# Output products of a recurrence grouped by their rows, and an order of TensorE that keeps products on parts of the array together

## The chip, the core and the metric

One Trainium2 chip, of which one core works. TensorE multiplies, VectorE (DVE), ScalarE (ACT) and GpSimd (POOL) do the elementwise work, and SyncE (SP) issues every DMA. The metric is the device time of one launch, in microseconds (us).

## The reference, cut to what matters

The function is one layer of a backbone, in float32, for 640 tokens (128 of a prompt and 512 of a sample):

```python
h = rms_norm(x, g_pre) * (1 + scale_m) + shift_m          # scale, shift, gate: c @ w_mod, 12288 values
proj = h @ w_in                                            # 2048 -> 5408
lru_out = rglru(conv(xl), forwards and backwards) * gelu(gl)
rwkv_out = wkv7(r, k, v, ..., forwards and backwards)      # 16 heads of 64, a recurrence over tokens
x = x + gate_m * rms_norm(concat(lru_out, rwkv_out) @ w_out)
x = x + gate_f * rms_norm((silu(h2 @ w_gate) * (h2 @ w_up)) @ w_down)   # hidden 5632
```

In `wkv7` each step updates a 64 x 64 state per head and reads it with `r`:

```python
sa = einsum('bhvk,bhk->bhv', S, -kk_t)
S = S * w_t + sa[..., None] * (kk_t * a_t) + v_t[..., None] * k_t
y_t = einsum('bhvk,bhk->bhv', S, r_t)
```

## The kernel before

**Stages.** Activations lie with channels on the 128 partitions and the 640 tokens along the free axis. First `x` is normalized. Then 43 row blocks of `w_in` are multiplied (accumulator `ps`), and beside them run the two recurrences. 16 row blocks of `w_out` follow: an early half that needs the first results of the mixers, and a late half with the rest. After the residual (`residual`, `right`) comes the feed-forward part, whose accumulators are `pb` and `pc`; it fills the second half of the launch.

**Dense products.** A weight tile is loaded into a buffer `raw` (256 KB, four of them; five more named `raw2` from the late half of `w_out` on), split into a coarse part and a rest (`w`, six buffers, by ACT, POOL and DVE), and multiplied with the split activations `hi` and `lo`: three products per tile and half of the tokens, each 128 rows by 128 columns of the array and 320 tokens long (function `main`, priority 9, the lowest). One load `raw` feeds 24 products.

**Modulation products.** `c @ w_mod` is worked off in between (`mod_main`, priority 8): pieces of `w_mod` land in the same `raw` buffers, two pieces make a group of four products. Each uses all 128 rows and 32 columns of the array, so that four of them run beside each other. They read `raw` directly, and the two buffers come free when the group is done.

**The recurrence.** It runs in chunks of 64 tokens for 8 pairs of heads and 2 directions, which makes 16 jobs (`chain`, priority 0). Each job has eight steps of three products (`pR`, `pU`, `pS`: tiles `pc<-svu,af`, `pc<-yy,rt`, `pc<-svu,bkt`), where each waits for DVE or ACT to copy the one before. At the end of a job come its outputs, in two halves of five chunks `c`. For a chunk there are two products with 128 rows and 64 columns (`svu` with `af`, one per head) and then two with 64 rows and 64 columns (`sa` with `ar`), accumulated into `py`. Preparing work (`elem`, `join`) has more products on parts of the array, 64 rows by 128 columns and 32 by 32.

**What sets the order.** The order of all engines is written by a list scheduler (`Sched`), at build time. Every stream (`chain`, `main`, `mod_main`, ...) offers its next operation with the time `s` at which it could start by the scheduler's own costs. `run` takes the smallest `s`; on the same engine a stream of a better priority goes first when it could start just as early. `array` gives the cost of a product. It calls a product whole when it uses all 128 rows and writes 128 partitions, and keeps in `mode` what the last one was. All operations are recorded through one helper line, so the profile shows L126 for each (L120 for DMAs): tiles tell them apart. At run time each engine goes through its list in that order and waits at the head of it.

Of the kernel before, what the change touches and what calls it, by code (L numbers as in the profile page):

```python
# [20 lines left out]
P = 128  # L21
# [14 lines left out]
CH = 64  # L36
# [5 lines left out]
H = (slice(0, 64), slice(64, 128))  # L42
# [3 lines left out]
WINDOW = 3.4133  # L46
SWITCH = 1.3
PATIENCE = 1.5
LAT = {
    "pe": {"pe": 0.0, "act": 0.2, "dve": 0.2, "pool": 0.2, "sync": 0.15},  # L50
    "act": {"pe": 0.29, "act": 0.14, "dve": 0.14, "pool": 0.17, "sync": 0.12},
# [126 lines left out]
        return t if r.dtype == F32 else t.bitcast(F32)  # L178


class Sched:


# [74 lines left out]
    def array(self, op, t):  # L258

        w = int(t / WINDOW)  # L260
        if w > self.win:
            if self.slow:
                self.slow = self.busy < 0.88 * WINDOW or w > self.win + 1
            else:
                self.slow = self.busy < 0.4 * WINDOW or w > self.win + 1
            self.win, self.busy = w, 0.0
        o, c = op.out, op.cost
        part = op.ins[0][1:3] + o[1:3]
        whole = (part[1] - part[0]) == P and (part[3] - part[2]) == P
        if whole or part in self.parts or (self.parts and part[1] - part[0] != self.parts[0][1] - self.parts[0][0]):  # L270
            self.parts = []
        if whole != self.mode:
            self.mode = whole
            c += 0.17
        if self.parts:
            c = 0.02
        elif self.slow:
            c *= 2
        if not whole:
            self.parts.append(part)  # L280
        self.busy += c
        return c
# [74 lines left out]
    def run(self, until=None):  # L357
        while self.streams and not (until is not None and until in self.ev):
            best = None
            cand = []  # L360
            for st in self.streams:
                h = st[2]
                if h is None:
                    continue
                if isinstance(h, Alt):
                    s, o, _ = min(((max(self.clk[o.eng], d), o, b) for (o, b), d in zip(h.ops, st[4])),
                                  key=lambda x: x[0] + x[1].cost + x[2])
                    ops = [o]
                else:
                    ops = h  # L370
                    s = max(self.clk[h[0].eng], st[4])
                sw = self.switch(ops[0])
                if sw and self.now - (min(st[4]) if isinstance(st[4], list) else st[4]) < PATIENCE:
                    s += sw
                cand.append((s, st, ops))
                if best is None or s < best[0]:
                    best = cand[-1]
            assert best is not None, "the streams wait for one another: %s" % [
                (st[0], st[1].__name__, st[1].gi_frame.f_lineno) for st in self.streams]
            eng = best[2][0].eng  # L380
            for c in cand:
                if c[1][0] < best[1][0] and c[2][0].eng == eng and c[0] <= best[0] + TOL[eng]:
                    best = c
                    break
            for op in best[2]:
                self.emit(op)
            self.step(best[1], None)
            self.poll()
# [29 lines left out]
class Step:  # L418
# [746 lines left out]
    def chain(self):  # L1165
        sc = self.sc
        blk = lambda t, i, h: t[H[h], i * P + h * CH:i * P + (h + 1) * CH]
        two = lambda out, src: Alt((self.copy(out, src), 0.0),
                                   (self.v.tensor_scalar(out, src, 1.0, 0.0, op0=ALU.mult, op1=ALU.add), 0.0))
        rt = yield self.take("rt")  # L1170
        for h in range(2):
            yield self.v.memset(rt[H[h], :, CH - h * CH:P - h * CH], 0.0)
        for n in range(NJ):
            p, d = n // 2, n % 2
            yield sc.wait(("I", n))
            jb = self.jobs[n]
            af, ar, pc, jt = jb["af"], jb["ar"], jb["pc"], jb["jt"]
            for r in jb["Q"]:
                yield self.move(rt[r, :, r], jt[r, :, 32:64])
            for ra, rb in jb["R"]:  # L1180
                yield self.v.memset(rt[rb, :, ra], 0.0)
                yield self.move(rt[ra, :, rb], jt[ra, :, 0:32])
            sc.rel(jt)
            tmp = yield self.take("yy")
            tmp_ = tmp.rearrange("p a b -> p (a b)").rearrange("p (a b) -> p a b", b=CH)
            sp, rs = tmp_[:, 0:2], tmp_[:, 2:4]
            sa = yield self.take("sa")
            pch = [0, 1] if d == 0 else [1, 0]
            sch = list(range(2, 10)) if d == 0 else list(range(9, 1, -1))
            cls = [[sch[j]] + ([pch[j]] if j < 2 else []) for j in range(8)]  # L1190
            yield self.v.memset(sa[:, pch[0], :], 0.0)
            yield self.q.dma_start(sa[:, sch[0], :], self.a["s0"][p, d])
            yield sc.wait(("V", p), ("B", n))
            svu, bkt = self.tiles["svu", p], jb["bkt"]
            for h in range(2):
                yield self.copy(af[H[h], :, 0, h, :], ar[H[h], :, 0, :])
            for c in cls[0]:
                yield self.copy(svu[0:64, 0, c, :], sa[0:64, c, :])
                yield self.copy(svu[64:128, 1, c, :], sa[64:128, c, :])
            for j in range(8):  # L1200
                cl = cls[j]
                m = len(cl)
                pR = yield self.take("pc")
                yield [self.mm(pR[:, i * P:(i + 1) * P], af[:, c, 0].rearrange("p h t -> p (h t)"), svu[:, :, c, :]) for i, c in enumerate(cl)]
                for h in range(2):
                    yield two(rs[H[h], 0:m], pR[H[h], 0:m * P].rearrange("p (i t) -> p i t", t=P)[:, :, h * CH:(h + 1) * CH])
                sc.rel(pR)
                pU = yield self.take("pc")
                yield [self.mm(pU[:, i * CH:(i + 1) * CH], rt[:, c], rs[:, i]) for i, c in enumerate(cl)]
                for i, c in enumerate(cl):  # L1210
                    for h in range(2):
                        yield two(svu[H[h], h, c, :], pU[H[h], i * CH:(i + 1) * CH])
                sc.rel(pU)
                if j == 7:
                    break
                for i, c in enumerate(cl):
                    yield self.s.activation(sp[:, i, :], sa[:, c, :], AF.Copy, scale=pc[:, c:c + 1])
                pS = yield self.take("pc")
                yield [self.mm(pS[:, i * P:(i + 1) * P], bkt[:, c, :], svu[:, :, c, :]) for i, c in enumerate(cl)]
                for i, c in enumerate(cl):  # L1220
                    f = pc[:, c:c + 1]
                    last = i == 1 and j == 1
                    cn = sch[j + 1] if i == 0 else pch[1]
                    for h in range(2):
                        yield self.stt(sp[H[h], i, :] if last else svu[H[h], h, cn, :], blk(pS, i, h), f[H[h]],
                                       sp[H[h], i, :])
                    if last:
                        yield self.q.dma_start(self.a["o_wkv"][p, d], sp[:, 1])
                        continue
                    for h in range(2):  # L1230
                        yield self.copy(sa[H[h], cn, :], svu[H[h], h, cn, :])
                sc.rel(pS)
            sc.rel(bkt, pc, tmp)
            yield sc.wait(("bonus", p))
            y = self.tiles["y", p]
            for half in range(2):
                py = yield self.any_of("pc", "pa")
                ops = []
                for c5 in range(5):
                    c = half * 5 + c5  # L1240
                    o = slice(c5 * CH, (c5 + 1) * CH)
                    ops += [self.mm(py[H[h], o], svu[:, h, c, :], af[:, c, 1, h, :], True, False) for h in range(2)] + \
                        [self.mm(py[H[h], o], sa[H[h], c, :], ar[H[h], c, 1, :], False, True) for h in range(2)]
                yield ops
                s = slice(half * NH, (half + 1) * NH)
                yield self.tt(y[:, s], py[:, 0:NH], y[:, s], ALU.add)
                sc.rel(py)
            sc.rel(af, ar, sa)
            if d == 1:
                sc.rel(svu)  # L1250
            sc.fire(("C", n))
# [774 lines left out]
```

## Time and profile before

| what | us |
|---|---|
| median of 3 runs (lowest, highest) | 3443.24 (3433.52, 3448.22) |
| the profiled execution, its own time | 3435.92 |
| its span, from the first to the last instruction | 3434.1 |
| TensorE busy in the span | 3261.4 |
| DVE busy in the span | 2214.1 |
| start, until 140 us: TensorE busy | 104.03 |
| recurrences, 140 to 1340 us: TensorE busy | 1147.59 |
| rest of `w_out`, 1340 to 1600 us: TensorE busy | 248.68 |
| residual, 1600 to 1728 us: TensorE busy, DVE busy | 85.19, 120.38 |
| feed-forward part, 1728 us to the end: TensorE busy | 1675.95 |

A product is recorded with its start and a modelled end, and products overlap; so the busy time of TensorE says little on how much room is left in it. The start of one product to the start of the next tells what a product costs in the stream. A float32 product stands as two records (the halves of the values), a split one (`hi`, `lo`, `w`) as one.

### The profile page before, as it was taken

How to read it: one execution, taken by the hardware profiler on the slowest of the kernel's cores; microseconds unless marked ns; L12 is line 12 of the kernel's file. 1: busy time of each engine (PE TensorE's matmuls, PEld its weight loads, DVE VectorE, ACT ScalarE, POOL GpSimd, SP SyncE). 2: the span in 40 equal slices, each digit the busy share in tenths (PEclk: the TensorE clock that was granted, in tenths of full speed). 3: DMA queues.
4: the chain of work that ended last, by engine and by line, in shares of the span. 5: the costliest groups of instructions: out<-in, count | busy, mean ns of one | idle time of the engine just before them, and what ended most of it. 6: DMA issues, size and time to landing. Idle time of an engine off the chain costs nothing.

```text
span 3434.1 us, 67033 instructions
## 1 busy us (share of the span) xinstructions
PE 3261.4 (95%) x25068; PEld 2895.7 (84%) x25068; DVE 2214.1 (64%) x3898; ACT 1543.8 (45%) x3254; POOL 1474.1 (43%) x1750
## 2 busy tenths in 40 slices
PE   6999999999999999998699999999999999999997
PEld 4787888888878877787499999999999988888885
DVE  4565667776766753157988888888888862323324
ACT  4435565656665655243444444444444432312323
POOL 1453345444444443436666666666565640000001
PEclk9999999999999999998799999999999999999998
DMA  9542333333333345784633333333333342423323
GB/s 372 181 108 76 88 105 102 99 102 106 98 100 89 95 147 170 215 272 147 212 90 102 100 100 96 102 102 99 97 102 102 98 147 77 136 78 104 97 77 132
DMA packets 262774, 422.56 MB, mean 123 GB/s; under 512 B 74800, under 2 KB 87728, under 8 KB 258352
## 3 DMA queue, kind: packets, MB, share of 16 engines
q1 hardware_dynamic: 262448, 418.27, 39.9%
q8 instruction: 198, 3.24, 0.4%
q14 instruction: 128, 1.05, 0.1%
HBM read 365.19 MB, written 52.96 MB: 122 GB/s over the span
## 4 chain that ended last, share of the span: by engine, by line
PE 72%; DVE 9%; DMA 3%; issue 2%; ACT 1%; POOL 0%; SPq 0%; DVEq 0%; POOLq 0%; ACTq 0%
PE pb L126 41%; PE ps L126 14%; PE pc L126 12%; PE pa L126 4%; DMA raw<-in_wmod_dram 2%; DVE pr L126 1%; PE pm L126 1%; DVE o L126 1%; DVE x L126 1%; DVE xl L126 1%; DVE svu L126 1%; DVE bk L126 1%; DVE hi L126 1%; DVE z L126 0%; DVE cf L126 0%
## 5 line engine op out<-in xcount | busy, mean ns | idle before, releaser
L126 PE MATMUL ps<-hi,w 128*128 128x320 f32 x3712 | 920.6, 325 | 9.7 <-ACT hi L126 7.8
L126 PEld LDWEIGHTS ps<-hi,w 128*128 128x128 f32 x3712 | 636.4, 191 | 59.5 <-issue 32.1
L126 PE MATMUL ps<-lo,w 128*128 128x320 f32 x1856 | 589.3, 324 | 1.3 <-POOL lo L126 0.9
L126 POOL TENSOR_TENSOR w<-raw,w 128x256 fp32r<-128x256 f32 x510 | 419.4, 823 | 183.4 <-ACT w L126 80.7
L126 POOL TENSOR_SCALAR w<-raw 128x256 fp32r<-128x256 f32 x408 | 200.1, 490 | 684.8 <-PE ps L126 572.3
L126 PEld LDWEIGHTS ps<-lo,w 128*128 128x128 f32 x1856 | 354.5, 191 | 22.0 <-issue 13.9
L126 POOL TENSOR_TENSOR hi<-raw 128x256 f32<-128x256 f32 (+1 forms) x348 | 309.9, 909 | 143.3 <-PE pb L126 122.6
L126 ACT ACTIVATE w<-raw 128x256 fp32r<-128x256 f32 x416 | 172.6, 415 | 362.9 <-PE pb L126 281.0
L126 POOL TENSOR_TENSOR lo<-raw 128x256 f32<-128x256 f32 (+1 forms) x216 | 223.6, 1043 | 234.6 <-PE pb L126 171.3
L126 PE MATMUL pb<-hi,lo 128*128 128x320 f32 (+1 forms) x931 | 271.5, 341 | 0.0
L126 PE MATMUL pb<-lo,lo 128*128 128x320 f32 (+1 forms) x835 | 252.7, 343 | 0.0
L126 DVE TENSOR_TENSOR w<-raw,w 128x256 fp32r<-128x256 f32 x314 | 184.1, 587 | 82.4 <-ACT w L126 52.7
L126 PE MATMUL pb<-hi,hi 128*128 128x320 f32 (+1 forms) x672 | 217.8, 343 | 0.0
L126 PE MATMUL pb<-o,hi 128*128 128x320 f32 x827 | 200.1, 310 | 2.4 <-DVE hi L126 1.2
L126 DVE TENSOR_TENSOR lo<-raw 128x128 f32<-128x128 f32 (+1 forms) x312 | 181.1, 612 | 0.0
L126 PEld LDWEIGHTS pb<-hi,lo 128*128 128x128 f32 x931 | 168.4, 189 | 13.5
L126 PE MATMUL pb<-o,lo 128*128 128x320 f32 x581 | 162.4, 311 | 1.5 <-DVE lo L126 1.5
L126 PE MATMUL pb<-lo,hi 128*128 128x512 f32 (+1 forms) x536 | 163.7, 353 | 0.0
L126 PEld LDWEIGHTS pb<-lo,lo 128*128 128x128 f32 x835 | 152.4, 189 | 12.6
L126 DVE TENSOR_TENSOR lo<-lo,hi 128x640 fp32r<-128x640 f32 (+1 forms) x121 | 115.5, 955 | 72.0 <-ACT hi L126 54.9
L126 PE MATMUL pb<-x,hi 128*128 128x320 f32 x655 | 158.3, 311 | 3.8 <-DVE hi L126 2.6
L126 PE MATMUL pb<-lo,w 128*128 128x320 f32 x528 | 161.7, 311 | 0.0
(402 smaller groups left out, 7733.3 us busy)
## 6 DMA issues: line engine op xcount, KB each, us to landing
raw<-in_w_gu_dram SPq DMA_DIRECT2D x352, 256.0 KB, 2.6
raw<-in_wmod_dram SPq DMA_DIRECT2D x256, 256.0 KB, 3.5
raw<-in_w_dn_dram SPq DMA_DIRECT2D x176, 256.0 KB, 2.6
raw<-in_w_in_dram SPq DMA_DIRECT2D x160, 256.0 KB, 3.3
mraw<-in_wmod_dram SPq DMA_DIRECT2D x32, 1024.0 KB, 11.2
raw<-in_w_out_dram SPq DMA_DIRECT2D x64, 256.0 KB, 3.9
gud<-z SPq DMA_DIRECT2D x44, 320.0 KB, 2.5
x<-in_xT_dram SPq DMA_DIRECT2D x32, 320.0 KB, 5.6
```

What stands on the lines that cost most here:

```text
L126: o = Op(eng, lambda: f(*args, **kw), _box(out), [_box(x) for x in ins], _cost(eng, op, out, ins), aset, 0)
```

## The change

Two things are changed. In `chain`, the outputs of a half are written in another order: first the ten products with 128 rows, for all five chunks, then the ten with 64 rows. Only the first and the last product of each kind now carry the marks for the start and the end of an accumulation. In the scheduler, an offered product of TensorE whose wholeness is not that of the last one gets 0.35 us added to its `s`: always when the last one used a part of the array, and when the last one was whole only for as long as the offered one has not been ready for `HOLD` (0) us, or for `HOLD_MOD` (8) us for streams of priority 8 and below, which are the modulation products. The cost of a change in `array` is 0.175 instead of 0.17.

```diff
+MODE, HOLD, HOLD_MOD = 0.35, 0.0, 8.0
...
+def whole(op):
+
+    return op.ins[0][2] - op.ins[0][1] == P and op.out[2] - op.out[1] == P
...
-        if whole != self.mode:
-            self.mode = whole
-            c += 0.17
+        if full != self.mode:
+            self.mode = full
+            c += MODE / 2
...
+                if ops[0].eng == "pe" and whole(ops[0]) != self.mode and (
+                        self.mode is False or self.now - st[4] < (HOLD if st[0] < 8 else HOLD_MOD)):
+                    s += MODE
...
-                    ops += [self.mm(py[H[h], o], svu[:, h, c, :], af[:, c, 1, h, :], True, False) for h in range(2)] + \
-                        [self.mm(py[H[h], o], sa[H[h], c, :], ar[H[h], c, 1, :], False, True) for h in range(2)]
+                    ops += [self.mm(py[H[h], o], svu[:, h, c, :], af[:, c, 1, h, :], c5 == 0, False) for h in range(2)]
+                for c5 in range(5):
+                    c = half * 5 + c5
+                    o = slice(c5 * CH, (c5 + 1) * CH)
+                    ops += [self.mm(py[H[h], o], sa[H[h], c, :], ar[H[h], c, 1, :], False, c5 == 4) for h in range(2)]
```

The scheduler writes the order of all engines up to the first products of the feed-forward part anew; from there on the rows of TensorE have the same shapes in the same order. Three places follow.

TensorE, the outputs of the first job, where the recurrence begins (`pc<-af,svu` and `pc<-ar,sa` are the two kinds of output products, `pa` holds products of other streams). Before:

```order
L126 MATMUL ps<-lo_1024,w 128x320
L126 MATMUL ps<-hi_1023,w 128x320 x2
L126 MATMUL pa<-c_ident,bk 128x128 x4
L126 MATMUL pc<-af,svu 64x64 x2
L126 MATMUL pc<-ar,sa 64x64 x2
```

and with the change:

```order
L127 MATMUL pc<-yy,rt 128x64
L127 MATMUL pa<-u,lruw 128x320
L127 MATMUL pa<-c_ident,bk 128x128 x4
L127 MATMUL pc<-af,svu 64x64 x10
L127 MATMUL pc<-ar,sa 64x64 x10
```

Before, the two rows of output products stand five times in turn for each half; now each kind stands once, with ten products.

TensorE, the early half of `w_out` (`raw` with `scv` are modulation products, `modsb` ends a block of them, `ps` is dense). Before:

```order
L126 MATMUL ps_17320<-lo8_15673,w_17321 128x320
L126 MATMUL pm_17269<-raw_17296,scv_191 32x256 x2
L126 MATMUL pm_17269<-raw_17315,scv_191 32x256 x2
L126 MATMUL ps_17320<-hi8_15672,w_17322 128x320 x2
L126 MATMUL ps_17320<-hi9_15822,w_17321 128x320
```

and with the change:

```order
L127 MATMUL ps_17283<-hi11_15634,w_17324 128x320 x2
L127 MATMUL pm_17087<-raw_17190,scv_191 32x256 x2
L127 MATMUL pm_17087<-raw_17268,scv_191 32x256 x2
L127 MATMUL pm_17087<-c_sel_249,modsb_17370 128x2 x2
L127 MATMUL pm_17388<-raw_17274,scv_191 32x256 x2
L127 MATMUL pm_17388<-raw_17335,scv_191 32x256 x2
L127 MATMUL ps_17402<-hi0_15031,w_17376 128x320
```

Where one group stood between dense products, two now stand almost together.

SP, the loads of the same two places (`in_wmod` is for modulation, `in_w_out` for dense products, the rest are results that go out and come back). Before:

```order
L120 DMA raw_17296<-in_wmod_dram 128x512
L120 DMA raw_17312<-in_w_out_dram 128x512
L120 DMA raw_17315<-in_wmod_dram 128x512
L120 DMA opd10_85<-gt_17319 128x640
L120 DMA mixd7_66<-lh_16765 128x640
```

and with the change:

```order
L121 DMA raw_17371<-in_wmod_dram 128x512
L121 DMA raw_17373<-in_w_out_dram 128x512
L121 DMA opd11_86<-gt_17363 128x640
L121 DMA lo12_17380<-mixd12_71 128x640
L121 DMA mixd15_74<-y_14385 128x640
L121 DMA raw_17394<-in_wmod_dram 128x512
L121 DMA raw_17396<-in_wmod_dram 128x512
L121 DMA raw_17405<-in_w_out_dram 128x512
```

With the change three pieces of `w_mod` (`raw_17371`, `raw_17394`, `raw_17396`) lie in three of the four buffers when the dense load `raw_17405` is issued, and in the program's list, where the engines' instructions stand in one order, only six dense products separate that load from the first product that reads it.

## Rows read from the trace of the kernel before

**Rows 1.** The page: busy time of each engine, and TensorE in 40 slices.

```profile
PE 3261.4 (95%) x25068; PEld 2895.7 (84%) x25068; DVE 2214.1 (64%) x3898; ACT 1543.8 (45%) x3254; POOL 1474.1 (43%) x1750
...
PE   6999999999999999998699999999999999999997
```

**Rows 2.** Stages: start:end, length, busy us of PE, PEld, DVE, ACT, POOL; clock, DMA.

```profile
400.00:700.00 300.00, 289.31 (x3288) 249.68 (x3288) 221.38 (x449) 185.66 (x448) 140.34 (x189) 0.99 0.36 100
...
1660.00:1728.00 68.00, 46.93 (x277) 33.40 (x278) 67.59 (x101) 32.53 (x71) 51.29 (x45) 0.75 0.55 175
1728.00:2000.00 272.00, 272.00 (x1858) 272.00 (x1857) 234.22 (x387) 117.50 (x222) 168.99 (x178) 1.00 0.33 98
```

**Rows 3.** TensorE in time: start us, us, tiles, records; outputs of one half.

```profile
285.09 0.34 PE L126 MATMUL pc<-af,svu 128*64 128x64 f32 x4
285.36 0.33 PE L126 MATMUL pc<-ar,sa 64*64 64x64 f32 x4
285.62 0.34 PE L126 MATMUL pc<-af,svu 128*64 128x64 f32 x4
...
287.72 0.44 PE L126 MATMUL pa<-c_ident,bk 128*128 128x128 f32 x2
```

**Rows 4.** TensorE in time: 16 records of one kind on half of the rows.

```profile
170.03 1.16 PE L126 MATMUL pa<-ar,bk 64*128 64x128 f32 x16
171.12 0.41 PE L126 MATMUL ps<-hi,w 128*128 128x320 f32 x1
```

**Rows 5.** TensorE in time: one modulation group (1420 us), two together (43 us).

```profile
1420.00 0.31 PE L126 MATMUL ps<-lo,w 128*128 128x320 f32 x1
1420.24 0.64 PE L126 MATMUL pc<-raw,scv 128*32 128x256 f32 x8
1420.81 0.42 PE L126 MATMUL ps<-hi,w 128*128 128x320 f32 x1
1421.07 0.31 PE L126 MATMUL ps<-lo,w 128*128 128x320 f32 x1
1421.21 0.60 PE L126 MATMUL ps<-hi,w 128*128 128x320 f32 x3
...
43.56 1.07 PE L126 MATMUL pc<-mraw,scv 128*32 128x256 f32 x16
44.56 0.38 PE L126 MATMUL pm<-c_sel,modsb 128*128 128x2 f32 x2
```

**Rows 6.** Groups, 1240 to 1600 us: busy us, mean ns, idle before, what ended it.

```profile
L126 PE MATMUL pm<-raw,scv 128*32 128x256 f32 x272 | 29.9, 401 | 9.6 <-DMA raw<-in_wmod_dram 7.7 <-issue 1.7
...
L126 PE MATMUL pc<-raw,scv 128*32 128x256 f32 x160 | 18.7, 393 | 4.4 <-DMA raw<-in_wmod_dram 4.3
```

**Rows 7.** DMA, 1240 to 1600 us, last row 200 to 1340: us to landing.

```profile
raw<-in_wmod_dram SPq DMA_DIRECT2D x109, 256.0 KB, 3.9
raw<-in_w_out_dram SPq DMA_DIRECT2D x62, 256.0 KB, 3.9
...
raw<-in_w_in_dram SPq DMA_DIRECT2D x143, 256.0 KB, 3.4
```

**Rows 8.** Groups, 1240 to 1600 us: splitting a load into coarse part and rest.

```profile
L126 POOL TENSOR_TENSOR w<-raw,w 128x256 fp32r<-128x256 f32 x95 | 77.8, 819 | 76.5 <-ACT w L126 59.5 <-PE ps L126 12.2
...
L126 ACT ACTIVATE w<-raw 128x256 fp32r<-128x256 f32 x42 | 17.6, 419 | 53.8 <-PE ps L126 52.0 <-DMA x<-in_xT_dram 1.3
```

**Rows 9.** Stretches as in the stages, around changes of the clock.

```profile
331.90:352.40 20.50, 17.18 (x264) 13.19 (x265) 11.04 (x20) 4.68 (x11) 4.56 (x3) 0.50 0.16 46
...
683.50:686.90 3.40, 3.20 (x118) 2.47 (x115) 0.90 (x3) 3.36 (x4) 0.00 (x0) 1.00 0.05 19
686.90:693.70 6.80, 6.80 (x50) 5.30 (x49) 3.83 (x8) 1.51 (x4) 0.62 (x1) 0.50 0.02 5
```

**Rows 10.** TensorE in time: idle us before the record, and what ended it.

```profile
333.40 0.76 PE L126 MATMUL pc<-svu,af 128*128 128x128 f32 x2 [3.27 <-DVE svu L126]
```

**Rows 11.** Waits of TensorE, 140 to 1600 us: us, times, longest.

```profile
PE pc L126 <- DVE svu L126: 15.5, 20, 3.3
```

More of the change, by code (lines that the diff above doesn't have):

```diff
@@ L268, in array @@
         part = op.ins[0][1:3] + o[1:3]
-        whole = (part[1] - part[0]) == P and (part[3] - part[2]) == P
-        if whole or part in self.parts or (self.parts and part[1] - part[0] != self.parts[0][1] - self.parts[0][0]):
+        full = whole(op)
+        if full or part in self.parts or (self.parts and part[1] - part[0] != self.parts[0][1] - self.parts[0][0]):
             self.parts = []
-        if whole != self.mode:
-            self.mode = whole
-            c += 0.17
+        if full != self.mode:
+            self.mode = full
+            c += MODE / 2
         if self.parts:
@@ L278, in array @@
             c *= 2
-        if not whole:
+        if not full:
             self.parts.append(part)
```

## The prediction

> **What bounds the kernel now.** The page shows TensorE busy for 95% of the span, with one dip in the 40 slices [rows 1]. The stages tell more. From 1728 us on TensorE is busy without a break (272.00 of 272.00 us) [rows 2]. Its products there have the same shapes in the same order with the change, so I take nothing from this half. In the residual, 1660 to 1728 us, DVE is the engine without room (67.59 of 68 us) [rows 2], and its work stays. What can move lies before 1600 us. There TensorE is nearly always busy (289.31 of 300 us from 400 to 700) [rows 2], and dense products of the lowest priority fill what the recurrence leaves. A faster group of products is therefore worth its time as long as dense products stand ready: the chain of the recurrence takes as long as before, and more dense work is done when it ends. Of waits, those in the chain for DVE are the largest in this part (15.5 us in 20 waits) [rows 11].
>
> **Outputs by number of rows.** A half takes 2.63 us from its first product to the next stream's (285.09 to 287.72), 0.53 us for each of five chunks [rows 3]. Four records of one kind start within 0.12 us (0.34 us less the 0.22 us that one lasts), and the other kind starts 0.27 us after them began [rows 3]. So 0.15 us of each 0.27 us goes between the kinds. Where kinds don't change, 16 records with 64 rows and 128 columns take 1.09 us to the next stream (170.03 to 171.12), that is 0.27 us for four, the leaving included [rows 4]; with half the columns to stream the four should take less. Bounds for four records followed by their own kind: 0.12 us (nothing between) and 0.27 us (nothing gained). I take 0.21, between them and nearer to the row, since the second pass over a column block has to wait for the first. A half then costs 10 x 0.21 + 2 x 0.05 = 2.2 us instead of 2.63, and 32 halves give 32 x 0.40 = **12.8 us less** (0 to 36).
>
> **Fewer entries into parts of the array.** Counted along the built order, TensorE goes from whole products to products on parts 322 times before and 258 times now; most of the 64 are modulation groups that now stand behind another group on parts. Alone, a group costs 0.24 us to its start, 0.57 to the next dense product and 0.26 to the one after (1420.00, .24, .81, 1421.07), where three dense starts lie 0.14 to 0.15 apart [rows 5]: 1.07 - 0.29 = 0.78 us. Two together take 1.00 us (43.56 to 44.56) instead of 0.57 [rows 5], so the pair costs 1.21 us instead of 1.56. That is 0.35 us for each entry saved, 64 x 0.35 = **22.4 us less** (10 to 25: where a group follows one of another shape, a change between shapes as in the outputs, 0.15 us, remains).
>
> **Modulation products wait less for their loads.** From 1240 to 1600 us there are 432 records, 54 groups; they are busy for 48.6 us and TensorE idles 12.0 us before them for the load [rows 6]. Undisturbed, a group is busy for 0.64 us [rows 5], 54 x 0.64 = 34.6. So 14.0 + 12.0 = 26 us go into waiting for pieces that take 3.9 us to land [rows 7]. Now a group may be passed over for up to 8 us. Counted along the program's list, with products costed by rows 3 to 5, 63 of 108 pieces of this part have less than 3.9 us of TensorE's work between issue and use before, and 10 of 106 now. I take 3 us of waiting as left: **23 us less** (13 to 26).
>
> **Dense loads wait more.** A piece that is passed over keeps one of the four `raw` buffers, and the dense load behind it is issued later. In the same count the 24 dense loads from the end of the recurrence to the start of the late half of `w_out` have 6.9 to 14.1 us of work between issue and first use before, none too few; now 0.6 to 8.4. What a load needs: 3.9 us to land [rows 7], 0.42 us for the coarse part, and 0.82 us for the rest [rows 8], which is first read four products (0.6 us) in: 4.6 us. 19 of the 24 fall short, by 35 us together, and one load earlier by 2: **37 us more**. If loads land in 3.4 us as in the recurrence [rows 7] and the rest is never late, they need 3.8 and the sum is 23; if nothing overlaps (3.9 + 0.42 + 0.82 = 5.2), it is 50. TensorE stands still then, and the chain of `w_out` products has nothing to hide it.
>
> **The clock.** At 683.50 to 686.90 TensorE is busy for 3.20 of 3.40 us, with products on parts alone, and at 686.90 its clock is granted at 0.50 (1.2 instead of 2.4 GHz) for 6.8 us [rows 9]. After an idle of 3.27 us [rows 10] it stayed at 0.50 for 20.5 us [rows 9]. At 1.2 GHz at most half of a stretch is lost. Longest runs of products on parts are, by the built order, 6.3 us and then 3.9 before; now four have 5 to 6 us: up to three more stretches of 6.8 us, 10 us. Six of the late loads leave over 3 us idle: six stretches of at least 3.4 us, 10 us. Both could also cost nothing, where a dense run follows at once. I take **8 us more** (0 to 20).
> The Trainium skill, "TensorE: Matmul & The Clock Gate", section "What's actually happening", says that the gate is set by how busy TensorE has recently been; by that, products on parts that follow each other closely would keep the clock, and the half of these 8 us that is for runs on parts would fall away. The row at 683.50 differs from it, and the measurement decides.
>
> **The chain itself.** With the same costs, the work that lies between its steps adds up to 151, 155 and 218 us (`pR` to `pU`, `pU` to `pS`, `pS` to `pR`) before, and to 156, 154 and 230 now. Its waits should stay: 0. SP's list has the same loads, and what is passed over there is the dense load that is counted above.
>
> **Sum.** -12.8 - 22.4 - 23 + 37 + 8 = -13.2 us. The profiled execution took 3435.9 us in all (span 3434.1), 7.3 under the median of the three runs, 3443.2. I put the sum on the median: **3430 us**, 0.4% less; a profile would show a span near 3421.
>
> **Rivals.**
> 1. Loads hidden. If loads are issued earlier than the list says, since SP runs ahead, the late loads cost 23 and the clock nothing: -12.8 - 22.4 - 23 + 23 = -35, 3408 us. For it: the loads that land in 3.4 us [rows 7]. Against it: the buffers, not SP, hold the loads back.
> 2. Starved `w_out`, slower than before. Modulation pieces parked in the `raw` buffers keep dense loads back at the full 5.2 us (50), and idle TensorE falls to 1.2 GHz (20 us): -58 + 70 = +12; if the waits for modulation stay half (13 more, as groups now run just before a load is due), +25: 3468 us. It decides from the point where late loads and clock together exceed 58 us. For it: an idle of 3.27 us before the clock fell [rows 10]. Against: nine buffers from the late half on.
> 3. The gain is not delivered. In the recurrence TensorE's list also waits for DVE [rows 11]; if each saved piece becomes a longer wait there, the 12.8 us and two thirds of the 22.4 go, and what is left is -8 - 23 + 37 + 8 = +14: 3457 us. Against it: the room between steps has not shrunk in the count.
>
> **How the numbers follow.** Forecast 0.45, with its own range of 12 us to both sides (3418 to 3442); rival 1 0.27, rival 2 0.16, rival 3 0.12. What a measurement of this kernel can tell from no change is about 0.5%, 17 us. Faster by more than that (under 3426): nearly all of rival 1 and a third of the forecast, 0.41. Slower (over 3460): two thirds of rival 2 and a part of rival 3, 0.16. Within: 0.43. The range from 3402 to 3462 leaves out the lower edge of rival 1 and the upper half of rival 2.
>
> **What would show it.** In a profile after: a half's outputs at 2.2 us instead of 2.63; modulation groups of 16 records and hardly an idle before them for their loads; `ps` products idle for a split of weights behind a load, about twenty times, between the end of the recurrence and the late half of `w_out`; the end of the last job at about the same time as before, with some 167 more dense products ahead of it, as the built order has them; the stretch from 1728 us on equally long. The forecast is wrong where `ps` does not wait there (rival 1), where it waits for over 50 us (rival 2), or where waits in the chain grow by 20 us (rival 3).

## The result

| | median us | lowest, highest | runs |
|---|---|---|---|
| before | 3443.0 | 3433.5, 3448.2 | 4 |
| after | 3408.4 | 3398.2, 3411.0 | 4 |

The ratio of after to before is 0.990, with a 95% interval of 0.987 to 0.993: 34.6 us less, 1.0%. The forecast was 3430 us, 0.4% less, with a range of 3402 to 3462. So the time lies inside the range and on the side of a clear gain, which had a chance of 0.41, and 22 us below the forecast. It is the number of rival 1 (3408), but not by the same terms, as the rows show.

The profiled execution of after took 3410.4 us, its span is 3408.6 (the prediction had 3421). First the busy times from the page of after, then its windows by stage: up to the last output of the recurrence, from there to the feed-forward part, and 272 us of this, as many as in [rows 2] (columns as there).

```profile
PE 3213.6 (94%) x25068; PEld 2892.3 (85%) x25068; DVE 2205.9 (65%) x3878; ACT 1541.9 (45%) x3282; POOL 1465.0 (43%) x1736
```

```profile
140.00:1339.00 1199.00, 1137.63 (x12133) 998.40 (x12133) 788.54 (x1671) 703.57 (x1701) 557.48 (x778) 0.96 0.39 108
1339.00:1725.60 386.60, 319.28 (x2194) 272.47 (x2191) 249.77 (x341) 158.01 (x320) 194.57 (x207) 0.86 0.62 198
...
1725.60:1997.60 272.00, 272.00 (x1856) 272.00 (x1856) 238.28 (x390) 115.16 (x220) 169.34 (x178) 1.00 0.33 100
```

The feed-forward part is as full as before (272.00 of 272 us, [rows 2]), and from the same product on (1751.5 us before, 1725.6 after) it takes TensorE 1658 us to its last product in both. So the whole change lies in front of it. The same two windows of before are:

```profile
140.00:1337.90 1197.90, 1145.47 (x11920) 978.83 (x11921) 796.97 (x1688) 693.78 (x1660) 543.64 (x757) 0.97 0.37 102
1337.90:1751.50 413.60, 359.46 (x2397) 295.28 (x2397) 251.24 (x340) 166.78 (x328) 220.38 (x246) 0.91 0.63 200
```

The last output of the recurrence comes at the same time (1337.9 and 1339.0 us), with 213 more records in the window ahead of it (11920 and 12133), and what is left after it takes 27 us less (413.6 and 386.6).

**Outputs.** TensorE in time, one half of the first job (as [rows 3]):

```profile
290.54 0.80 PE L127 MATMUL pc<-af,svu 128*64 128x64 f32 x20
291.27 0.80 PE L127 MATMUL pc<-ar,sa 64*64 64x64 f32 x20
292.00 0.80 PE L127 MATMUL pa<-u,lruw 32*128 32x320 f32 x2
```

Twenty records of one kind take 0.73 us to the next row. A half costs 1.46 us and not the 2.2 of the prediction; before it was 2.63. The single records in the trace show where the rest goes: within a kind they start 7 and 52 ns apart in turn, 117 ns for four, and at a change of kind the next record starts 148 to 152 ns later, after which one step takes 100 ns instead of 52. Both orders pay this at each change of kind, the old one ten times in a half and the new one twice.

**Modulation.** Groups, 1240 to 1575 us (as [rows 6]):

```profile
L127 PE MATMUL pm<-raw,scv 128*32 128x256 f32 x280 | 21.1, 394 | 1.7 <-DMA raw<-in_wmod_dram 1.4 <-ACT mod L127 0.4
...
L127 PE MATMUL pc<-raw,scv 128*32 128x256 f32 x128 | 9.9, 386 | 0.5 <-DMA raw<-in_wmod_dram 0.5
```

These 408 records, 51 groups, are busy for 31.0 us, 0.61 us each, and TensorE idles 2.2 us before them, 1.9 of it for loads. In [rows 6] it was 48.6 us for 54, and 14.0 us of idle, 12.0 of it for loads.

**Waits of TensorE**, 140 to 1600 us (us, times, longest; as [rows 11]):

```profile
PE ps L127 <- POOL w L127: 17.9, 16, 4.1
PE pa L127 <- issue: 12.0, 7, 3.0
PE pa L127 <- DVE jt L127: 6.6, 5, 2.3
PE pa L127 <- DMA lruw<-in_lruw_dram: 6.4, 4, 2.5
PE pc L127 <- DVE svu L127: 5.1, 9, 1.3
PE pb L127 <- DVE st L127: 3.8, 1, 3.8
PE ps L127 <- ACT w L127: 3.8, 2, 2.4
```

and of before, the one for the split of weights:

```profile
PE ps L126 <- POOL w L126: 0.4, 1, 0.4
```

Against before, the largest wait of the chain went from 15.5 us in 20 waits [rows 11] to 5.1 in 9. Dense products now wait 18 times for a split of weights, 21.7 us in all, where they waited once for 0.4 us before. And the products that prepare the recurrence and the gates (`pa`) wait more: for their own loads (`lruw`), for DVE (`jt`), and for nothing that the profile shows ("issue"; before 5.6 us in 5 waits).

**The account.** The table sums the distances from start to start along TensorE's list up to the first 6000 dense products, which all kernels here have in common: up to 1751.5 us before and 1725.6 after. Each change of product has the price that it has in the trace of before at the full clock. What is over that price is a wait, put down to the product that comes late; outputs stand with what they took. At the half clock all that is over the price stands in the last row. A wait during which the clock fell counts as a wait; put to the half clock instead, the change of the dense products is about +21 and that of the half clock about +38, with nearly the same sum. Dense products are here `ps` and, after the last output, the first `pb` products too.

| us | before | after | change | predicted |
|---|---|---|---|---|
| outputs | 88.0 | 53.1 | -34.9 | -12.8 |
| rest of the list by price | 1394.2 | 1371.7 | -22.5 | -22.4 |
| waits, modulation products | 40.0 | 9.6 | -30.4 | -23 |
| waits, dense products | 20.0 | 53.7 | +33.7 | +37 |
| waits, chain | 40.4 | 18.3 | -22.1 | 0 |
| waits, other products | 57.1 | 82.1 | +25.0 | 0 |
| more at the half clock | 89.5 | 114.5 | +25.0 | +8 |
| sum | 1729.2 | 1702.8 | -26.4 | -13.2 |

The second row is a price list and not a measurement of its own; what it leaves out shows in the waits. The account is of one execution of each kernel: by the medians after takes 34.6 us less, in the two traces 26.4. The granted clock of whole executions, which most runs have on record, goes with this. It was 0.974 in the traced execution of before and 0.972 on average over 42 others; in after it was 0.966 in the traced one and 0.967 on average over five. The span times what the clock lacks to 1 estimates the loss: 27 us more in after by the two traces, 13 us by the averages.

### The profile page after: what moved, and what is told of

It reads as the page before. It is cut to its first block, busy times and chain, and to the rows that moved or that the text cites. A ratio compares the mean times of both kernels' runs of the same rounds, so it can differ in the third digit from the quotient of the medians.

```text
span 3408.6 us, 67001 instructions
## 1 busy us (share of the span) xinstructions
PE 3213.6 (94%) x25068; PEld 2892.3 (85%) x25068; DVE 2205.9 (65%) x3878; ACT 1541.9 (45%) x3282; POOL 1465.0 (43%) x1736
## 4 chain that ended last, share of the span: by engine, by line
PE 80%; DVE 9%; DMA 6%; issue 2%; ACT 2%; SPq 1%; POOL 1%; DVEq 0%; POOLq 0%; ACTq 0%
PE pb L127 41%; PE ps L127 19%; PE pc L127 11%; PE pa L127 6%; DMA raw<-in_w_out_dram 2%; PE pm L127 2%; DVE pr L127 1%; DVE x L127 1%; DVE o L127 1%; SPq L121 1%; DVE lo L127 1%; DMA raw<-in_wmod_dram 1%; DVE xl L127 1%; DVE hi L127 1%; DVE u L127 1%
## 5 line engine op out<-in xcount | busy, mean ns | idle before, releaser
L127 POOL TENSOR_TENSOR hi<-raw 128x256 f32<-128x256 f32 (+1 forms) x307 | 291.6, 966 | 208.1 <-PE pb L127 188.4
L127 POOL TENSOR_TENSOR lo<-raw 128x256 f32<-128x256 f32 (+1 forms) x260 | 241.7, 943 | 171.6 <-PE pb L127 107.3
L127 PE MATMUL pb<-hi,lo 128*128 128x320 f32 (+1 forms) x984 | 292.4, 339 | 0.0
L127 PE MATMUL pb<-lo,lo 128*128 128x512 f32 (+1 forms) x646 | 204.3, 356 | 0.0
L127 PE MATMUL pb<-lo,hi 128*128 128x320 f32 (+1 forms) x604 | 189.9, 346 | 0.0
L127 PE MATMUL pb<-x,lo 128*128 128x320 f32 x774 | 172.0, 310 | 2.7 <-DVE x L127 2.1
L127 PE MATMUL pb<-o,hi 128*128 128x320 f32 x726 | 173.8, 309 | 0.0
L127 PE MATMUL pb<-o,w 128*128 128x320 f32 x792 | 160.8, 311 | 0.4 <-DVE w L127 0.4
L127 DVE TENSOR_TENSOR lo<-raw 128x256 f32<-128x256 f32 (+1 forms) x268 | 157.3, 611 | 0.0
L127 DVE TENSOR_TENSOR hi<-raw 128x256 f32<-128x256 f32 (+1 forms) x221 | 145.6, 681 | 0.0
```

The source lines that it names most:

```text
L127: o = Op(eng, lambda: f(*args, **kw), _box(out), [_box(x) for x in ins], _cost(eng, op, out, ins), aset, 0)
```

## The experiments

The same account for the experiments, from one trace each. Traced executions need not lie at the median: that of enter_free took 3369.4 us, that of no_hold 3410.7 and that of rule_only 3416.5. "Waits of the recurrence" are those of the chain and of other products together.

| kernel | median us | outputs | list | modulation | dense | recurrence | half clock | sum |
|---|---|---|---|---|---|---|---|---|
| before | 3443 | 88 | 1394 | 40 | 20 | 97 | 89 | 1729 |
| after | 3408 | 53 | 1372 | 10 | 54 | 100 | 115 | 1703 |
| after_again | 3399 (one run) | 54 | 1372 | 10 | 48 | 100 | 110 | 1693 |
| group_only | 3403 | 53 | 1394 | 39 | 21 | 101 | 85 | 1694 |
| rule_only | 3429 | 90 | 1372 | 11 | 48 | 99 | 91 | 1710 |
| rule_only_again | 3439 (one run) | 90 | 1372 | 9 | 50 | 94 | 118 | 1732 |
| enter_free | 3379 | 54 | 1384 | 35 | 28 | 94 | 67 | 1662 |
| no_hold | 3397 | 51 | 1381 | 31 | 27 | 118 | 92 | 1701 |
| hold_mod_only | 3395 | 54 | 1375 | 22 | 48 | 98 | 95 | 1691 |
| no_keep | 3384 | 52 | 1373 | 11 | 48 | 103 | 86 | 1674 |
| mod_rate_1 | 3384 | 52 | 1370 | 13 | 44 | 112 | 88 | 1678 |
| keep_050 | 3424 | 53 | 1383 | 50 | 25 | 109 | 99 | 1719 |
| keep_030 | 3406 | 53 | 1383 | 59 | 23 | 93 | 88 | 1698 |
| no_keep_rate_1 | 3392 | 53 | 1373 | 27 | 34 | 111 | 87 | 1684 |

### The two edits apart

Theory A came from the equal time of the last output: the recurrence's own chain sets the pace, and savings there turn into waits. Theory B is the prediction's: each piece counts by its own price.

**group_only** is the kernel before with the outputs in the new order:

```diff
-                    ops += [self.mm(py[H[h], o], svu[:, h, c, :], af[:, c, 1, h, :], True, False) for h in range(2)] + \
...
+                    ops += [self.mm(py[H[h], o], svu[:, h, c, :], af[:, c, 1, h, :], c5 == 0, False) for h in range(2)]
+                for c5 in range(5):
...
```

> The kernel before with its outputs grouped by rows and nothing else; the order of all other products stays, and 4371 dense products stand ahead of the last job's last output, as before. Theory A (up to the last output the recurrence's own chain sets the time, and TensorE's waits there are what is left over): the 12.8 us saved on outputs turn into waits in the chain (40 us in the kernel before, then some 53), the last output stays at 1338 us, and the kernel takes as long as before, 3443 us, ratio 0.999 to 1.001. Theory B (each piece of TensorE's list counts by its own price, as the prediction's sum had it): the last output comes at 1325 us, the kernel takes 13 us less, 3430, ratio 0.996. Both expect a half at 2.2 us.

Measured: 3402.8 us against 3441.4, ratio 0.988 (0.986 to 0.990), 39 us less. Theory A falls, as TensorE in time shows at the last outputs:

```profile
1294.89 0.80 PE L126 MATMUL pc<-af,svu 128*64 128x64 f32 x20
1295.62 0.80 PE L126 MATMUL pc<-ar,sa 64*64 64x64 f32 x20
1296.35 0.41 PE L126 MATMUL ps<-lo,w 128*128 128x320 f32 x1
```

They end at 1296 us and not at 1338, and the waits of the recurrence hardly grew (97 to 101, where A had 13 more). The mechanism is B's, at nearly three times its price: 34.7 us for the outputs, and no other part moved by over 7. The new order also moves products that add into the same columns away from each other, but that is not what saves the time: the first `ar` product of a half follows an `af` product of another column block now, and still starts 152 ns after it, as it did before, when it followed the one of its own block.

**rule_only** is the changed kernel with the outputs in the old order.

> The changed kernel with its outputs in the old order: the scheduler's rule alone. The order of the rest is that of the changed kernel (4538 dense products ahead of the last output). Theory A: the 13 us that the old outputs cost are taken out of the waits in the chain (18 us in the changed kernel), the last output stays at 1339 us and the time within 4 us of the changed kernel's, 3405 to 3412. Theory B: the last output comes 13 us later, near 1352, and the kernel takes 3421 us.

Measured: 3428.9 us, ratio 0.997 (0.995 to 0.999): 12 us less than before, 20 more than after. The last output comes at 1350 us, as B had it; the time is above both expectations, since the outputs cost 36 us more than in after and not 13. So each edit gains alone, and together they bring no more than the grouping alone: on top of it the rule adds 6 us by the medians, which the intervals don't tell from nothing. The runs of rule_only lie far apart (3416.5 to 3452.9), which two more runs look into below.

### The clauses of the rule

**enter_free**: products on parts are never put off.

```diff
-                if ops[0].eng == "pe" and whole(ops[0]) != self.mode and (
-                        self.mode is False or self.now - st[4] < (HOLD if st[0] < 8 else HOLD_MOD)):
+                if ops[0].eng == "pe" and whole(ops[0]) != self.mode and self.mode is False:
```

> The changed kernel where the rule keeps TensorE on products on parts but never puts off going to them. By the built order it makes 304 entries instead of 258, 4361 dense products stand ahead of the last output (4371 in the kernel before), and priced by the kernel before TensorE's list up to there is 25 us shorter than before. Theory A: the last output stays at 1338 us, the tail has 2 us more of work than in the kernel before, so no gain: 3440 to 3447 us. Theory B: the last output comes near 1313 us and the kernel takes about 3420. Both: hardly a dense product waits for a load in the tail (under 8 us), modulation products wait as in the kernel before (some 29 us).

Measured: 3378.7 us, ratio 0.981 (0.979 to 0.983), the fastest of all: 63 us under before, 30 under after. The last output comes before 1270 us, and not at 1338, and up to there the granted clock is 0.99 (0.96 in after). TensorE in time, and the window:

```profile
1269.13 0.80 PE L127 MATMUL pc<-ar,sa 64*64 64x64 f32 x20
```

```profile
140.00:1269.70 1129.70, 1081.48 (x11896) 943.66 (x11896) 792.93 (x1675) 689.90 (x1685) 520.18 (x735) 0.99 0.39 109
```

Theory A falls once more. B with the outputs at their measured price (22 us more) would give 3398; the other 19 are about what the half clock gives back (67 us in place of 89). After the last output modulation products wait 26.0 us in the account, where some 29 were expected, and the row of the dense products has 12.8. These are waits of `pb` for the residual's results: no `ps` product idles there, as expected (under 8 us for loads).

**no_hold**: modulation groups are put off no longer.

```diff
-MODE, HOLD, HOLD_MOD = 0.35, 0.0, 8.0
+MODE, HOLD, HOLD_MOD = 0.35, 0.0, 0.0
```

> The changed kernel with the 8 us for which a modulation group may be put off set to 0. 300 entries, 4518 dense products ahead of the last output. By the count of work between issue and use no dense load falls short (37 us in the changed kernel), modulation loads fall short by 23 us (3 in the changed kernel). Theory A: the last output at 1338 us, after it 286.5 us of products and 99 us of waits and slow clock as in the kernel before: 28 us under the kernel before, 3415 us. Theory B: the list is 25.6 us shorter than before and the waits as before: 3417 us. Both: dense waits in the tail under 8 us (27.5 in the changed kernel), modulation waits there 20 to 29 us (7.7).

Measured: 3397.1 us, ratio 0.987 (0.984 to 0.989). The waits are as expected: after the last output 3.1 us of dense waits and 25.1 of modulation waits. No `ps` product idles for a split of weights after the last output. So the groups that are put off are what starves the dense loads, and the 8 us trade one wait for the other: without them, dense waits fall by 26 us against after and modulation waits rise by 22. B's 3417 less the 22 of the outputs is 3395.

**hold_mod_only**: of the products on parts only modulation groups are put off.

```diff
-MODE, HOLD, HOLD_MOD = 0.35, 0.0, 8.0
+MODE, HOLD, HOLD_MOD = 0.35, -1e9, 8.0
```

> The changed kernel where the rule still puts off modulation groups (up to 8 us) but never puts off the recurrence's and the gates' products. Theory C (putting off products of the recurrence is what makes the changed kernel slower than the one with free entry, 3408 against 3379 us): the waits and the slow clock up to the last output fall as between no_hold and enter_free, 18 us: 3390 us. Theory D (the modulation groups that are put off cost it, through the dense loads behind them): still 3405 to 3420 us, with 27 us or more of dense waits in the tail, since by the count of work between issue and use the dense loads fall short by 46 us instead of 37.

Measured: 3395.4 us, ratio 0.988 (0.986 to 0.990), 13 under after. Neither theory has it alone: the time is near C's, but the dense waits after the last output stay (29.9 us), as D had it. What fell against after is the half clock (95 for 115) and the waits of other products in the recurrence, and the last output comes at 1314 us.

**no_keep**: only entering is put off.

```diff
-                        self.mode is False or self.now - st[4] < (HOLD if st[0] < 8 else HOLD_MOD)):
+                        self.now - st[4] < (HOLD if st[0] < 8 else HOLD_MOD)):
```

> The changed kernel without the clause that keeps TensorE on products on parts: only entering is put off. It makes 263 entries (258 in the changed kernel), and 4573 dense products stand ahead of the last output (4538). Theory E (that clause is what gives enter_free its 24 us over group_only): it is missed here too, 3425 to 3435 us. Theory F (the gain follows the number of entries and the loads that fall short, whichever clause brings them): entries cost 2 us more, dense and modulation loads fall short by 39 us instead of 40: 3405 to 3412 us.

Measured: 3383.8 us, ratio 0.984 (0.983 to 0.986). Both theories missed it, E by over 40 us. Each of the two clauses (keeping TensorE on parts, putting off entries) alone, on top of the grouping, takes about 20 us off (3379 and 3384 against 3403); both together take nothing off. Against after, the list and the modulation waits are the same within 2 us, dense waits fall by 5, and the half clock falls by 28 (115 to 86).

### Late dense loads

**mod_rate_1** spreads the modulation pieces more thinly over the dense loads:

```diff
-MOD_RATE, MOD_RATE2 = 0.55, 1.8
+MOD_RATE, MOD_RATE2 = 0.55, 1.0
```

> The changed kernel with the modulation pieces spread more thinly over the dense loads of the early half of w_out (1.0 for each instead of 1.8). By the count of work between issue and use the dense loads fall short by 21 us instead of 37, modulation loads by 4 instead of 3; 254 entries instead of 258. If the dense waits of the changed kernel come from its loads' late issue: dense waits after the last output near 12 us instead of 27, and 15 to 20 us less in all, 3388 to 3393 us. If they come from elsewhere (splits, the engines' order): no change, 3404 to 3412 us.

Measured: 3383.7 us, ratio 0.983 (0.981 to 0.986), 25 under after. That is more than the expectation, but only in part by its mechanism: dense waits after the last output fell from 27.5 to 22.7 us only, not to 12. Of these, idle time for a split of weights fell from 16.4 to 10.2 us. The half clock there fell from 65 to 44. The count of work between issue and use is thus too coarse to tell where single loads come late, and for the change itself its sum was too large (37 us, for 21.3 more of idle behind splits).

### How far a new order moves the time by itself

**keep_050** and **keep_030** are enter_free with another price for leaving products on parts (0.50 and 0.30; the cost of a change in `array` is half of it and goes with it), **no_keep_rate_1** is no_keep and mod_rate_1 together.

```diff
-MODE, HOLD, HOLD_MOD = 0.35, 0.0, 8.0
+MODE, HOLD, HOLD_MOD = 0.5, -1e9, -1e9
```

> The kernel with free entry, with the price of leaving products on parts raised from 0.35 to 0.50 us. By the built order 302 entries instead of 304, the recurrence is favoured more: 4250 dense products ahead of the last output instead of 4361, the list as long as before (1458 us up to the residual, by rows' prices). If only the list's sum and its loads count: 3376 to 3382 us, as enter_free. If it counts that the recurrence ends early, so that its waits and the slow clock fall further: 3365 us or less. If the list of the tail, with more modulation groups among fewer dense products, costs it: 3390 us.

> The kernel with free entry, with the price of leaving products on parts at 0.30 us instead of 0.35 (keep_050 raised it and took 3424 us). By the built order 310 entries instead of 304, 4541 dense products ahead of the last output instead of 4361, the list up to the residual at 1457.6 us by rows' prices (1458.5), loads short by 27 us (24). If the count decides: 3377 to 3385 us. If the price shifts the time steadily (keep_050 was 45 us slower): 3365 to 3370. If a new order by itself moves the time: 3390 us or more, with the difference in waits and slow clock and not in the list.

> No_keep and mod_rate_1 together: TensorE isn't kept on products on parts, only entering is put off, and the modulation pieces are spread at 1.0 for each dense load. 261 entries, 4601 dense products ahead of the last output; by the count of work between issue and use dense loads fall short by 5 us and modulation loads by 20, 14 us less than in no_keep (39). If the two edits add up: 3365 to 3375 us, the fastest so far. If what no_keep and mod_rate_1 gained is the scatter of a new order of the list: anywhere from 3370 to 3420.

Measured: 3424.2 (ratio 0.996, 0.995 to 0.998), 3406.1 (0.990, 0.989 to 0.992) and 3391.8 us (0.986, 0.984 to 0.987). A price a little higher and one a little lower cost enter_free 45 and 27 us, with the list within 2 us of its own. Modulation waits grew by 15 and 24 us and the half clock by 32 and 21. The two edits that gained 25 us each over after give 17 together. Some of this is the traced execution of enter_free, which was 9 us faster than its median. So a new order of the list moves this kernel by tens of us through waits and clock that neither the list nor the count of loads shows.

**after_again** and **rule_only_again** are the same two programs once more, for their traces.

> The changed kernel once more, for its trace alone. Up to the residual's end the extra time at the half clock was 115 us in its first trace and 91 in the trace of rule_only, whose list is the same but for the outputs. If the order of the list sets it: 110 to 120 us again. If it scatters between executions of one program: anywhere from 90 to 130, with the rest of the waits within 5 us of the first trace.

> Rule_only once more, for its trace alone. Its first trace was of an execution that took 14 us less than its median. If the half clock scatters between executions of one program: more than the 91 us of the first trace, 95 to 125. If the list sets it: 86 to 96 again.

Measured: in after the half clock took 110 us in the second trace, 115 in the first. The granted clock of its five executions on record is 0.966 to 0.970, below every execution of group_only, no_keep and enter_free (0.971 to 0.981). So the greater loss in after is no chance of one execution. In rule_only it took 118 us, and 91 in the first trace: one program, the waits at full clock within 3 us for each kind, and 22 us of difference in the time. Its twelve executions have clocks from 0.964 to 0.974, and the slowest (3452.9 us) has the lowest, the fastest (3416.5) the highest. Rule_only up to its last output, in its two executions (the third figure from the end is the granted clock):

```profile
140.00:1349.90 1209.90, 1156.29 (x12132) 1002.49 (x12130) 787.35 (x1670) 703.66 (x1700) 558.49 (x779) 0.98 0.38 107
```

```profile
140.00:1367.90 1227.90, 1175.61 (x12144) 1019.73 (x12145) 792.37 (x1675) 705.34 (x1701) 565.47 (x781) 0.96 0.38 106
```

## Why the prediction was right in its sum, and where it was not

1. **Outputs: the term was mis-sized, -12.8 for -34.9.** For four records followed by their own kind it had bounds of 0.12 and 0.27 us and took 0.21, since the second pass over a column block "has to wait for the first". No such wait shows: within a kind four records take 117 ns, which is the lower bound, and with the changes of kind 20 take 0.73 us, 0.146 for four. The lower bound, read from the starts of records of one kind in [rows 3], was the better guide, and each change of kind adds the 0.15 us that the prediction had read there, where its sum put 0.05. The row with 64 rows and 128 columns [rows 4] was not like this one. (2.63 less 2.2 is also 0.43 and not the 0.40 that it multiplied, 1 us in 32 halves.) Group_only shows it without the rule.
2. **Fewer entries: as far as shown, right.** Along the list the 64 entries are worth 22.5 us by the prices of [rows 5]. That is counted, not measured by itself.
3. **Modulation waits: right, a little small** (-30 for -23). 1.9 us of waiting for loads are left in the stretch of [rows 6], where 3 were put.
4. **Dense loads: the mechanism was right, the term too large.** The account's row has +34 for +37, but not all of it is late loads. The idle time for a split of weights, which is what a late load leaves, grew by 21.3 us (0.4 to 21.7); the rest of the row are waits for results of DVE and of the residual. `ps` waits 18 times for a split, as "about twenty" had it, but only 11 of these, 16.4 us, after the last output, where nearly all of the 37 were put. No_hold shows the cause: without the 8 us, no `ps` product waits for a split there.
5. **The chain: the step failed.** Its waits "should stay", by the room between its steps. They fell by 22 us. But waits of other products rose by 25, and chain and others together hardly changed (97 and 100 us). They went from `svu` to `pa` products, whose loads and DVE steps now come late.
6. **The clock: right in sign, mis-sized** (+25 for +8 in the two traces, about +13 by the clocks of all executions on record). Of the 25 us, 15 lie after the last output, where the late loads are that the prediction counted. The other 10 lie in the recurrence, and for these it had counted long runs on parts. The rows there show more often a `pa` product that is late, as here (TensorE in time, then two windows, each with the granted clock third from the end):

```profile
847.95 0.69 PE L127 MATMUL pa<-jt,yj 32*32 32x16 f32 x60
851.31 0.51 PE L127 MATMUL pa<-jt,yj 32*32 32x16 f32 x20 [2.67 <-issue]
```

```profile
846.80:850.20 3.40, 1.84 (x69) 1.39 (x66) 0.34 (x1) 2.98 (x4) 0.40 (x1) 1.00 0.54 148
850.70:860.90 10.20, 9.59 (x87) 8.76 (x87) 5.89 (x10) 5.76 (x8) 2.43 (x3) 0.50 0.10 28
```

TensorE is busy for 1.84 of 3.40 us and idles 2.67 us before the second row; the clock falls near the end of this idle (850.7 us) and stands at 1.2 GHz for 10.2 us. From 140 us to the last output, idles of over 2 us number 3 before and 9 and 4 in the two traces of after, with 72, 96 and 89 us at the half clock. Of the nine, seven stand before a `pa` product, and beside seven the clock falls within 2 us.

7. **The sum** was 13 us off in the trace's account (-26 for -13): 22 us of the outputs and 7 of the modulation not counted, against 17 of the clock, and small rests. By the medians it was 22 off, as much as the outputs alone, in line with a clock that took less in after's other executions. That it was off by no more is luck in part: the late loads were put 16 us too high, while other waits of dense products were put at nothing, and the chain's 22 us less meet 25 more of other products.

Rival 1 gave the time, and its 23 us for late loads come near the 21.3 of the rows. But its reason is not shown: it took loads that land in 3.4 us, and after the last output those of `w_out` land in 4.6. Its clock at nothing is 13 to 25 us here, and the outputs, which it took from the forecast, make up for it. Rival 2's mechanism is there, but short of its point of decision (58 us): the waits for splits and the half clock together add 34 to 46 us. Rival 3 is refuted by group_only: saved time on outputs comes out as time.

Open is why after loses 28 us more to the half clock than no_keep and 48 more than enter_free (18 and 37 by the clocks of all their executions). The number of long idles goes with it only roughly: in rule_only, 5 and 7 of them came with 51 and 95 us. No experiment here sets the clock apart from the order.

## What to carry to other kernels

Products that run beside each other on parts of the array are worth sorting by kind where they can be: the time between kinds is nearly all gained, and the starts of neighbouring records of one kind give its price. A rule for a list scheduler is to be judged by several of its variants on the chip and not by what it counts: here the variants with grouped outputs and the rule, whose lists lie within 15 us, took between 3379 and 3424 us, and the best of them (the grouping with products on parts never put off, 3379 us) beats both kernels. Something put off to save changes of mode keeps its buffers too, so that what waits for these buffers belongs into the sum.

## What was not expected of the hardware

- Twenty records of one kind with 64 columns take 0.73 us to the next kind, 37 ns for each, with 128 and with 64 rows alike; changing kinds every four records made it 0.53 us for eight [rows 3]. Within a kind it is 29 ns for each; the rest belongs to the change.
- One program lost 91 us to the half clock in one execution and 118 in another (rule_only), with its other waits alike.
- An idle of 2.67 us within the recurrence came with a fall of the clock and 10.2 us at 1.2 GHz, though TensorE was busy for 9.59 us of these.
